# D's first key and query stacks made when their projections are complete, and the norms that begin a layer summing their squares on TensorE

## The chip, the cores and the metric

The kernel runs on one core of a Trainium2 chip. The metric is the device time of one execution in microseconds (us), lower is better. The engines of the core named here are TensorE (PE in the profile, with PEld for its weight loads), VectorE (DVE), ScalarE (ACT), GpSimd (POOL) and SyncE (SP), which here only issues DMAs.

## The reference

A trunk of two layers on 768 tokens of 1024 channels: 512 of a prompt and 256 of a sample, which don't see each other. All is fp32. One layer is, in the reference's own words:

```python
def _rmsnorm(x, gain):
    xf = x.astype(jnp.float32)
    xf = xf * lax.rsqrt(jnp.mean(xf * xf, axis=-1, keepdims=True) + EPS)
    return (xf * gain.astype(jnp.float32)).astype(x.dtype)
...
# sandwich RMSNorm -> one input projection split among four token mixers
#   A: 2-D neighbourhood attention with a learned position bias
#   B: grouped-query attention, normalised q and k, 2-D axial rotary positions
#   C: differential attention with ALiBi
#   D: sliding-window grouped-query attention, learned sink logit and ALiBi
# -> a projection per branch -> sigmoid gates, one per branch -> output projection
# -> post RMSNorm -> residual add; then a gated ConvFFN between two RMSNorms
```

D has four query heads of 64 channels and two key heads; a query sees keys at most 128 tokens away:

```python
logits = jnp.einsum('bqkgd,bskd->bkgqs', q_blk, k).astype(jnp.float32) * scale
logits = logits - sl[None, :, :, None, None] * rel.astype(jnp.float32)[None, None, None]
logits = jnp.where(valid[None, None, None], logits, NEG_INF)
sink_col = jnp.broadcast_to(sk[None, :, :, None, None], logits.shape[:-1] + (1,))
p = jax.nn.softmax(jnp.concatenate([logits, sink_col], axis=-1), axis=-1)[..., :-1]
```

## The kernel before, in words

**Data and products.** Channels lie on the 128 partitions, tokens along the free dimension. A norm works on one group of 256 tokens at a time (G0, G1, G2), as four tiles of 128 x 2 x 256 (two blocks of channels each; the profile writes 128x512). A product of two fp32 matrices is made of three passes with split operands: each operand is cut into a rounded high part (a copy on ACT) and what is left (a subtraction on DVE). So each weight, each normalised activation `h`, and each stack of keys or queries costs a copy on ACT and a subtraction on DVE before TensorE can use it. All products are issued by the helper at L460, transposes and broadcasts by transpose at L464, ACT's operations at L476, DVE's at L490, L494 and L499, the rsqrt on POOL at L505, DMAs at L509. A row with one of these lines is known by its tiles: `w` a weight, `raw` the same as loaded, `h` the activation, `g` general buffers (stacks, sums), `p` buffers of 128 x 512, `b` and `d` PSUM: four banks of 512 words (`b`) and two blocks of 1024 (`d`).

**A norm** (`pre_norm`, L713). ACT squares the four tiles of a group; DVE adds the second, third and fourth square to the first (three adds of 128 x 512); `mean_square` (L700) multiplies the sum by a column of ones on TensorE, four matmuls of 128 x 2 in fp32, which the profile shows as eight. DVE and POOL make the reciprocal root, TensorE spreads it over the partitions with two transposes, DVE multiplies the tiles by it, ACT copies them to `h` and DVE subtracts to get what is left. Six norms begin a layer: one for each of three token groups in the two layers. Layer 0's are made by `first_norm` (L760) from tiles loaded from DRAM. Layer 1's belong to the end of layer 0's FFN (`sandwich`, L772), where a first norm of the FFN's output, the residual add and the next layer's `pre_norm` follow one another. The other norms (inside a layer, before the FFN) go through the same `pre_norm` with `easy` set; the change leaves them as they are.

**A layer's attention part.** The list `JOBS` sets the order: first V of B and D with, in the same job, the keys of D and the first queries of D (`AHEAD`), one token group after another; then an early gate `t` (the first is A5: 48 products of 128x512 form of `h` with a weight from the bias buffers); then `job_D`, and the others. In `job_V` (L1797) the two blocks `k` and `q` of D are complete after G2 and put into `begun`; `proj` (L950) hands them out when `job_D` (L1864) asks for them, after the early gate. `job_D` then starts the tasks that make the stacks: `k_stack` (L985) copies each half of the block, subtracts, and sends the result to the other half of the partitions by DMA; `q_stack` is a copy and a scaled subtraction. Each of the two `d` blocks is free again when its stack is made. `job_D` then projects the second queries (q1) into a `d` block and starts the heads.

**What sets the order.** The order on each engine is not written out: a planner (class `Flow`, L243) runs the jobs as tasks at build time, with a clock per engine and a cost estimate per instruction, and emits an instruction whenever a task reaches it. A task with a lower number goes first; a `yield t` lets the task sleep until the planned time t. So a change to one task can move instructions of all later ones. On the chip, each engine runs its instructions in the order so written and waits on semaphores.

## Time and profile before

| what | value |
|---|---|
| median of 3 runs | 2510.05 us (2509.87 to 2511.64) |
| the profiled execution | 2509.31 us, its span 2507.5 us |
| mean granted TensorE clock | 0.993 |
| TensorE busy | 2451.6 us, 98% |
| VectorE busy | 1715.7 us, 68% |
| ScalarE busy | 1279.4 us, 51% |

The span goes from the first to the last instruction of the core; the execution's own time is 1.8 us longer. A row of the timeline is one instruction or a run of equal ones: start, length, engine, line, operation, tiles out<-in, shapes, count, and in brackets how long the engine stood idle before it and what released it. Lengths on TensorE overlap a little, since its matmuls are pipelined. The granted clock is a share of full speed: 1.00 is 2.4 GHz, 0.50 is 1.2 GHz.

### The profile page before, as it was taken

The page shows a single profiled execution, that of the slowest core. Times are in us where ns is not written, and L with a number is a line of the kernel's source. Part 1 is how long each engine was busy: PE and PEld are TensorE (multiplying, and loading weights), DVE is VectorE, ACT ScalarE, POOL GpSimd, SP SyncE. Part 2 cuts the span into 40 slices and gives each one's busy share as a digit, 9 for nine tenths or more (in the row PEclk, how much of TensorE's full clock was granted, in tenths as well). Part 3 has the DMA queues.
Part 4 walks back from the last instruction along what each step waited for, and adds up shares of the span by engine and source line. Part 5 has one row for each costly group of instructions (what it writes and reads, how often), then busy time and mean ns, then how long its engine had stood idle before and what let it go on. Part 6 is the DMA issues. An engine that isn't in the chain of part 4 may idle for free.

```text
span 2507.5 us, 40408 instructions
## 1 busy us (share of the span) xinstructions
PE 2451.6 (98%) x15486; PEld 2275.7 (91%) x15486; DVE 1715.7 (68%) x3278; ACT 1279.4 (51%) x2492; POOL 39.7 (2%) x38
## 2 busy tenths in 40 slices
PE   7999999999999999999989999999999999999998
PEld 7898888888999999988889988888889999999887
DVE  5567567736467888776766675676464679887866
ACT  5565655622355655563555645655224555556533
POOL 0001000000000000000000010000000000000000
PEclk9999999999999999999999999999999999999999
DMA  3443355343333333363334432544333233433643
GB/s 126 128 118 102 93 159 142 106 144 120 102 110 122 111 112 108 100 230 124 127 110 118 126 104 81 162 129 141 135 102 125 84 124 114 121 117 125 196 142 105
DMA packets 164273, 309.92 MB, mean 124 GB/s; under 512 B 25968, under 2 KB 90096, under 8 KB 164080
## 3 DMA queue, kind: packets, MB, share of 16 engines
q1 hardware_dynamic: 164080, 307.34, 39.7%
q8 instruction: 122, 2.00, 0.3%
q14 instruction: 71, 0.58, 0.1%
HBM read 225.74 MB, written 62.65 MB: 115 GB/s over the span
## 4 chain that ended last, share of the span: by engine, by line
PE 46%; DVE 2%; ACT 2%; issue 1%; DMA 1%; POOLq 0%; DVEq 0%; ACTq 0%
PE d L460 31%; PE b L460 15%; PE b L464 1%; DVE g L490 1%; ACT g L476 1%; DVE p L490 0%; DMA raw<-weights 0%; ACT p L476 0%; DVE h L490 0%; ACT s L476 0%; ACT w L476 0%; DVE w L490 0%; DMA bi<-alibi 0%; DVE bi L490 0%; ACT bi L476 0%
## 5 line engine op out<-in xcount | busy, mean ns | idle before, releaser
L460 PE MATMUL d<-h,w 128*128 128x256 f32 (+2 forms) x5400 | 989.9, 335 | 10.5 <-DVE g L490 8.7
L460 PEld LDWEIGHTS d<-h,w 128*128 128x128 f32 x5400 | 825.1, 190 | 103.1 <-issue 11.4
L460 PE MATMUL d<-g,w 128*128 128x256 f32 (+2 forms) x2547 | 443.7, 330 | 2.0 <-ACT g L476 1.5
L460 PEld LDWEIGHTS d<-g,w 128*128 128x128 f32 x2547 | 398.9, 188 | 33.0 <-ACT g L476 4.2
L490 DVE TENSOR_TENSOR w<-raw,w 128x1024 fp32r<-128x1024 f32 (+3 forms) x216 | 238.2, 1104 | 230.7 <-ACT w L476 224.5
L476 ACT ACTIVATE w<-raw 128x1024 fp32r<-128x1024 f32 (+3 forms) x216 | 206.8, 959 | 122.2 <-PE d L460 71.0
L476 ACT ACTIVATE p<-p,st 128x256 f32<-128x256 f32 (+2 forms) x288 | 175.0, 613 | 151.8 <-DVE st L499 94.5
L460 PE MATMUL b<-h,w 128*128 128x384 f32 (+2 forms) x1272 | 223.8, 330 | 0.0
L460 PEld LDWEIGHTS b<-h,w 128*128 128x128 f32 x1272 | 203.6, 188 | 10.3
L460 PE MATMUL b<-g,w 128*128 128x384 f32 (+2 forms) x1233 | 207.3, 322 | 0.0
L476 ACT ACTIVATE g<-d 128x384 f32<-128x384 f32 (+6 forms) x200 | 105.3, 534 | 185.6 <-PE d L460 157.6
L460 PEld LDWEIGHTS b<-g,w 128*128 128x128 f32 x1233 | 197.9, 189 | 1.6
L490 DVE TENSOR_TENSOR g<-g,b 128x512 f32<-128x512 f32 (+2 forms) x178 | 104.5, 599 | 66.0 <-PE b L460 45.8
L494 DVE SCALAR_TENSOR_TENSOR p<-g,par,p 128x511 f32<-128x511 f32 (+1 forms) x224 | 137.4, 615 | 8.9 <-ACT p L476 5.0
L476 ACT ACTIVATE p<-b 128x512 fp32r<-128x512 f32 (+3 forms) x172 | 91.9, 541 | 91.0 <-PE b L464 75.7
L490 DVE TENSOR_TENSOR p<-b,p 128x512 fp32r<-128x512 f32 (+1 forms) x162 | 100.3, 630 | 42.6 <-ACT p L476 41.8
L490 DVE TENSOR_TENSOR g<-g,d 128x768 f32<-128x768 f32 (+2 forms) x114 | 77.8, 686 | 70.1 <-PE d L460 70.1
L476 ACT ACTIVATE g<-p 128x512 fp32r<-128x512 f32 (+1 forms) x116 | 66.4, 574 | 93.4 <-DVE p L490 59.3
L460 PE MATMUL b<-g,g 128*128 128x512 f32 (+2 forms) x384 | 105.7, 346 | 5.4 <-DVE st L1157 3.6
L476 ACT ACTIVATE p<-g,par 128x512 f32<-128x512 f32 (+1 forms) x112 | 78.7, 703 | 50.3 <-DVE g L490 49.5
L1157 DVE CUSTOM_DVE_ANT_0 p<-b,bi 128x512 f32<-128x512 f32 (+2 forms) x144 | 81.6, 567 | 25.7 <-PE b L460 16.6
L460 PE MATMUL b<-p,g 128*128 128x256 f32 x576 | 95.8, 288 | 2.3 <-DVE p L490 1.5
(119 smaller groups left out, 3116.1 us busy)
## 6 DMA issues: line engine op xcount, KB each, us to landing
raw<-weights SPq DMA_DIRECT2D x206, 512.0 KB, 3.8
bi<-weights SPq DMA_DIRECT2D x48, 512.0 KB, 4.2
g<-g SPq DMA_DIRECT2D x128, 96.0 KB, 2.3
p<-v SPq DMA_DIRECT2D x44, 256.0 KB, 3.7
x<-g SPq DMA_DIRECT2D x36, 256.0 KB, 2.2
p<-x SPq DMA_DIRECT2D x36, 256.0 KB, 4.4
v<-p SPq DMA_DIRECT2D x28, 256.0 KB, 2.0
p<-x_in SPq DMA_DIRECT2D x24, 256.0 KB, 4.6
```

The costliest lines, as they stand in the source:

```text
L460: self.nc.tensor.matmul(out=out, lhsT=lhsT, rhs=rhs, start=start, stop=stop, skip_group_check=more)
L464: self.nc.tensor.transpose(out=out, in_=in_, identity=self.ident)
L476: self.nc.scalar.activation(out=out, in_=in_, func=func, **k)
L490: self.nc.vector.tensor_tensor(out=out, in0=a, in1=b, op=op)
L494: self.nc.vector.scalar_tensor_tensor(out=out, in0=a, scalar=s, in1=b, op0=op0, op1=op1)
L1157: nc.vector.tensor_tensor_reduce(out=p[:, :nkey], in0=s[:, :nkey], in1=bt, scale=1.0, scalar=init, op0=ALU.add, op1=ALU.max, accum_out=mx[ ...
```

## The change

Two things change. In `pre_norm` without `easy`, that is in the six norms that begin a layer, each square goes straight to TensorE as a `mean_square` of its own: four groups that accumulate into the same PSUM bank, in place of three adds on DVE and one group. And the stacks of D's keys and first queries are started inside `job_V`, when the last token group of their projection is through, in place of being handed to `job_D`; `job_D` keeps only the second queries.

```diff
--- before.py
+++ after.py
@@ -725,16 +725,19 @@
             if first:
                 yield t
             t = q.t = self.act(q.ap, ap, AF.Square, t, q.t)
-            if i:
-                if first:
-                    yield t
+            if not easy:
+                yield t
+                t = self.mean_square(b, q.ap, not i, i == len(x) - 1, t)
+                q.drop(t)
+            elif i:
                 t = sq.t = self.tt(sq.ap, sq.ap, q.ap, ALU.add, t, sq.t)
                 q.drop(t)
             else:
                 sq = q
-        yield t
-        t = self.mean_square(b, sq.ap, True, True, t)
-        sq.drop(t)
+        if easy:
+            yield t
+            t = self.mean_square(b, sq.ap, True, True, t)
+            sq.drop(t)
         yield t
         r = self.rstd_bcast(b, 2, t)
         tn = next(r)
@@ -948,8 +951,6 @@
         return out
 
     def proj(self, kind, name, m):
-        if (kind, name, m) in self.begun:
-            return self.begun.pop((kind, name, m))
         w = yield from self.weight((kind, name, m))
         blk = yield from self.dblock()
         blk.t = yield from self.mblock(self.whole(blk), w, self.h_rhs(self.h), KB)
@@ -1818,7 +1819,7 @@
                 blk.t = yield from self.mblock([(blk.cols(c0, c0 + GRP), c0, c0 + GRP)], w, self.h_rhs(self.h), KB)
                 if G == 2:
                     w.drop()
-                    self.begun[key] = blk
+                    self.f.start(self.queries_D(blk, 0) if n else self.keys_D(blk), 0)
         for w in ws:
             w.drop()
 
@@ -1861,26 +1862,21 @@
             blk = yield from self.proj("q", "B", m)
             self.f.start(queries(blk, m), 0)
 
+    def keys_D(self, blk):
+        ks = yield from self.k_stack(blk.full, blk.t, 6)
+        blk.drop(ks[1].t - 2000)
+        self.d_keys.extend(ks)
+
+    def queries_D(self, blk, m):
+        q = yield from self.q_stack(blk.full, 0.125, blk.t, 6)
+        blk.drop(q.t)
+        while not self.d_keys:
+            yield self.f.now + 200
+        self.heads("D", (2 * m, 2 * m + 1), lambda h: (q, self.d_keys[m], self.v["BD"][1], None))
+
     def job_D(self, _):
-        kbox = []
-
-        def keys(blk):
-            ks = yield from self.k_stack(blk.full, blk.t, 6)
-            blk.drop(ks[1].t - 2000)
-            kbox.extend(ks)
-
-        def queries(blk, m):
-            q = yield from self.q_stack(blk.full, 0.125, blk.t, 6)
-            blk.drop(q.t)
-            while not kbox:
-                yield self.f.now + 200
-            self.heads("D", (2 * m, 2 * m + 1), lambda h: (q, kbox[m], self.v["BD"][1], None))
-
-        blk = yield from self.proj("k", "D", 0)
-        self.f.start(keys(blk), 0)
-        for m in range(2):
-            blk = yield from self.proj("q", "D", m)
-            self.f.start(queries(blk, m), 0)
+        blk = yield from self.proj("q", "D", 1)
+        self.f.start(self.queries_D(blk, 1), 0)
 
     def job_C(self, m):
         part, m = m[0], int(m[1])
@@ -1898,7 +1894,7 @@
 
     def layer(self, l):
         self.l = l
-        self.begun = {}
+        self.d_keys = []
         self.par = self.pars[l]
         self.queue, self.bias_queue, self.att_end = [], [], False
         self.f.start(self.bias_loader(), 1)
```

The order shows three places. First ACT in layer 0 around the early gate A5 (the last row `p` <- `b` pair is A5's output, `d` are the blocks of D's keys and queries, `g` their stacks, `w` weights). Before:

```order
L476 ACTIVATE w_584<-raw_251 128x1024
L476 ACTIVATE lam_610<-lam_610 128x2
L476 ACTIVATE w_627<-raw_303 128x1024
L476 ACTIVATE w_650<-raw_590 128x1024
L476 ACTIVATE w_673<-raw_636 128x1024
L476 ACTIVATE p_685<-b_619 128x512
L476 ACTIVATE g_687<-d_287 64x768
L476 ACTIVATE g_691<-d_287 64x768
L476 ACTIVATE g_695<-d_335 64x768 x2
L476 ACTIVATE p_708<-b_620 128x256
```

and after:

```order
L476 ACTIVATE g_609<-d_323 64x768
L476 ACTIVATE g_613<-d_323 64x768
L476 ACTIVATE w_619<-raw_262 128x1024
L476 ACTIVATE lam_645<-lam_645 128x2
L476 ACTIVATE g_658<-d_360 64x768 x2
L476 ACTIVATE w_667<-raw_340 128x1024
L476 ACTIVATE w_696<-raw_625 128x1024
L476 ACTIVATE p_723<-b_654 128x512
L476 ACTIVATE p_737<-b_655 128x256
```

The copies of D's stacks stood behind A5's output and now stand ahead of it: k's two ahead of the weight copies, q's pair between them.

The second is the start of the program on TensorE (`const` with two columns: the sums of squares; `h_93` the first normalised activation, `st` the broadcast). Before:

```order
L460 MATMUL b_130<-const,p_131 128x2 x4
L464 MATMUL b_130<-const,st_146 128x128 x2
L460 MATMUL d_197<-w_157,h_93 128x256 x12
L460 MATMUL d_197<-w_179,h_93 128x256 x12
L460 MATMUL b_118<-const,p_119 128x2 x4
L460 MATMUL d_241<-w_157,h_93 128x256 x12
L460 MATMUL d_241<-w_179,h_93 128x256 x12
```

and after:

```order
L460 MATMUL b_130<-const,p_131 128x2 x4
L460 MATMUL b_130<-const,p_137 128x2 x4
L460 MATMUL b_130<-const,p_143 128x2 x4
L460 MATMUL b_130<-const,p_149 128x2 x4
L464 MATMUL b_130<-const,st_155 128x128 x2
L460 MATMUL b_118<-const,p_119 128x2 x4
L460 MATMUL b_118<-const,p_195 128x2 x4
L460 MATMUL b_203<-const,p_204 128x2 x4
L460 MATMUL d_219<-w_166,h_93 128x256 x6
L460 MATMUL b_118<-const,p_210 128x2 x4
L460 MATMUL d_219<-w_166,h_93 128x256 x6
L460 MATMUL d_219<-w_186,h_93 128x256 x6
```

One group for G0 became four; two groups of G1 (p_119, p_195) and one of G2 (p_204) now stand ahead of the first product of V (d_219).

ACT at the same place, where p_1xx and p_2xx are the squares and h_93 the copies of the activation. Before:

```order
L476 ACTIVATE w_157<-raw_106 128x1024
L476 ACTIVATE p_119<-p_110 128x512
L476 ACTIVATE h_93<-p_94 128x2x256
L476 ACTIVATE h_93<-p_96 128x2x256
L476 ACTIVATE h_93<-p_98 128x2x256
L476 ACTIVATE h_93<-p_100 128x2x256
L476 ACTIVATE p_165<-p_112 128x512
L476 ACTIVATE w_179<-raw_108 128x1024
L476 ACTIVATE p_185<-p_114 128x512
L476 ACTIVATE p_192<-p_116 128x512
```

and after:

```order
L476 ACTIVATE w_166<-raw_106 128x1024
L476 ACTIVATE h_93<-p_94 128x2x256
L476 ACTIVATE h_93<-p_96 128x2x256
L476 ACTIVATE h_93<-p_98 128x2x256
L476 ACTIVATE h_93<-p_100 128x2x256
L476 ACTIVATE p_119<-p_110 128x512
L476 ACTIVATE w_186<-raw_108 128x1024
L476 ACTIVATE p_195<-p_112 128x512
L476 ACTIVATE p_204<-p_120 128x512
L476 ACTIVATE p_210<-p_114 128x512
```

The squares of G1 and G2 moved behind the four copies of `h` and behind the second weight.

The third is the boundary of the layers on TensorE, at the norms of G1 and G2 (b with `const`: sums of squares; `b_13082`, `b_13111` and `b_13134`: V of G1). Before:

```order
L460 MATMUL d_12989<-h_11743,w_12842 128x256 x12
L460 MATMUL d_13031<-h_11743,w_12868 128x256 x7
L464 MATMUL b_12911<-const,st_12993 128x128 x2
L460 MATMUL d_13031<-h_11743,w_12868 128x256 x17
L460 MATMUL b_13082<-w_12282,h_11743 128x256 x12
L460 MATMUL b_13082<-w_12332,h_11743 128x256 x12
L460 MATMUL b_13111<-w_12282,h_11743 128x256 x12
L460 MATMUL b_13111<-w_12332,h_11743 128x256 x12
L460 MATMUL b_13056<-const,p_13057 128x2 x4
```

and after:

```order
L460 MATMUL d_13060<-h_11768,w_12905 128x256 x11
L464 MATMUL b_12941<-const,st_13024 128x128 x2
L460 MATMUL d_13060<-h_11768,w_12905 128x256
L464 MATMUL b_12774<-const,st_13030 128x128 x2
L460 MATMUL d_13060<-h_11768,w_12905 128x256 x12
L460 MATMUL b_13089<-const,p_13090 128x2 x4
L460 MATMUL b_13089<-const,p_13120 128x2 x4
L460 MATMUL b_13089<-const,p_13126 128x2 x4
L460 MATMUL b_13134<-w_12307,h_11768 128x256 x6
L460 MATMUL b_13089<-const,p_13132 128x2 x4
L460 MATMUL b_13134<-w_12307,h_11768 128x256 x6
L460 MATMUL b_13134<-w_12357,h_11768 128x256 x12
```

Three groups of G2's norm now stand ahead of V of G1, and one in the middle of it, where the only one stood behind two blocks of V.

And DVE there, where `p` as a second input is the old sum that is added. Before:

```order
L499 TENSOR_SCALAR st_12993<-b_12911 128x2
L490 TENSOR_TENSOR g_10899<-g_10899,b_12830 128x2x256
L490 TENSOR_TENSOR g_10950<-g_10950,b_12830 128x2x256
L490 TENSOR_TENSOR g_11006<-g_11006,b_12830 128x2x256
L490 TENSOR_TENSOR g_11057<-g_11057,b_12830 128x2x256
L490 TENSOR_TENSOR h_11743<-g_10899,h_11743 128x2x256
L490 TENSOR_TENSOR h_11743<-g_10950,h_11743 128x2x256
L490 TENSOR_TENSOR h_11743<-g_11006,h_11743 128x2x256
L490 TENSOR_TENSOR h_11743<-g_11057,h_11743 128x2x256
L490 TENSOR_TENSOR g_10899<-g_10899,b_12911 128x2x256
L490 TENSOR_TENSOR g_10899<-g_10899,p_12903 128x2x256
```

and after:

```order
L499 TENSOR_SCALAR st_13024<-b_12941 128x2
L499 TENSOR_SCALAR st_13030<-b_12774 128x2
L490 TENSOR_TENSOR g_10924<-g_10924,b_12941 128x2x256
L490 TENSOR_TENSOR g_10924<-g_10924,p_12933 128x2x256
L490 TENSOR_TENSOR g_10975<-g_10975,b_12941 128x2x256
L490 TENSOR_TENSOR g_10975<-g_10975,p_12935 128x2x256
L490 TENSOR_TENSOR g_11031<-g_11031,b_12941 128x2x256
L490 TENSOR_TENSOR g_11031<-g_11031,p_12937 128x2x256
L490 TENSOR_TENSOR g_11082<-g_11082,b_12941 128x2x256
L490 TENSOR_TENSOR g_11082<-g_11082,p_12939 128x2x256
L490 TENSOR_TENSOR g_10924<-g_10924,b_12774 128x2x256
L490 TENSOR_TENSOR g_10975<-g_10975,b_12774 128x2x256
```

Of the two norms that end together, the multiplications of G1's norm and its subtractions into `h` stood ahead of the pairs of multiply and add for G2; now the four pairs stand ahead.

## Rows read from the trace of the kernel before

**Rows 1.** The page: the span, and busy time of each engine.

```profile
span 2507.5 us, 40408 instructions
...
PE 2451.6 (98%) x15486; PEld 2275.7 (91%) x15486; DVE 1715.7 (68%) x3278; ACT 1279.4 (51%) x2492; POOL 39.7 (2%) x38
```

**Rows 2.** What TensorE waited for, whole span: total us, times, longest us.

```profile
PE b L460 <- DVE p L490: 21.3, 18, 8.6
...
PE d L460 <- DVE g L490: 9.1, 4, 4.2
```

**Rows 3.** Timeline of TensorE, layer 0: start, length, form, count [idle before, releaser].

```profile
60.61 8.64 PE L460 MATMUL b<-h,bi 128*128 128x512 f32 x48
...
73.43 4.93 PE L460 MATMUL d<-h,w 128*128 128x512 f32 x18 [4.17 <-DVE g L490]
...
80.77 4.67 PE L460 MATMUL d<-h,w 128*128 128x512 f32 x26
```

**Rows 4.** Timeline of TensorE, the same place in layer 1.

```profile
1305.16 8.64 PE L460 MATMUL b<-h,bi 128*128 128x512 f32 x48
...
1317.97 5.90 PE L460 MATMUL d<-h,w 128*128 128x512 f32 x18 [4.17 <-DVE g L490]
```

**Rows 5.** Windows on TensorE: us, busy (count), granted clock, DMA share, GB/s.

```profile
16.30:60.60 44.30, 41.01 (x307) 0.96 0.24 75
...
73.40:78.20 4.80, 4.77 (x18) 0.64 0.94 213
...
1228.40:1278.90 50.50, 44.18 (x326) 0.90 0.36 115
...
1278.90:1305.20 26.30, 24.51 (x204) 1.00 0.17 55
...
1318.00:1323.70 5.70, 5.70 (x18) 0.52 0.94 242
```

**Rows 6.** Timeline of the other engines beside A5, layer 0.

```profile
69.67 0.79 ACT L476 ACTIVATE g<-d 64x768 fp32r<-64x768 f32 x1
...
71.47 2.32 SPq L509 DMA_DIRECT2D g<-g  x2
...
75.14 0.96 DVE L494 SCALAR_TENSOR_TENSOR g<-d,g 64x768 fp32r<-64x768 f32 x1 [0.87 <-ACT g L476]
```

**Rows 7.** Timeline of the first 24 us.

```profile
2.76 0.47 SPq L509 DMA_DIRECT2D const<-const  x1
...
8.57 1.86 PE L460 MATMUL b<-const,p 128*128 128x2 f32 x8 [8.57 <-DVE p L490]
...
11.46 0.69 PE L464 MATMUL b<-const,st 128*128 128x128 f32 x2 [1.03 <-POOL st L505]
...
13.18 2.47 DVE L490 TENSOR_TENSOR p<-p,b 128x512 f32<-128x512 f32 x4
...
13.95 2.42 ACT L476 ACTIVATE h<-p 128x512 fp32r<-128x512 f32 x4 [1.43 <-DVE p L490]
...
16.31 4.54 PE L460 MATMUL d<-w,h 128*128 128x256 f32 x23 [1.10 <-DVE h L490]
...
21.45 1.05 PE L460 MATMUL b<-const,p 128*128 128x2 f32 x8 [0.59 <-DVE p L490]
```

**Rows 8.** Timeline of ACT in the same stretch.

```profile
16.28 0.61 ACT L476 ACTIVATE p<-p 128x512 f32<-128x512 f32 x1
...
16.80 1.04 ACT L476 ACTIVATE w<-raw 128x1024 fp32r<-128x1024 f32 x1
```

**Rows 9.** DMA issues of the first 60 us: count, KB each, us to landing.

```profile
const<-const SPq DMA_DIRECT2D x1, 72.0 KB, 4.5
```

**Rows 10.** Timeline of TensorE and DVE at the layer boundary.

```profile
1261.23 1.15 PE L460 MATMUL b<-const,p 128*128 128x2 f32 x8 [2.29 <-DVE p L490]
...
1278.97 0.68 DVE L490 TENSOR_TENSOR g<-g,b 128x512 f32<-128x512 f32 x1
...
1284.27 2.28 DVE L490 TENSOR_TENSOR p<-p,p 128x512 f32<-128x512 f32 x3
```

## The prediction

> **What bounds the kernel now.** I read the page first: TensorE is busy for 2451.6 us of a span of 2507.5 us [rows 1]. That is 55.9 us of idle time in all, so an edit that leaves TensorE's work alone can gain no more than that, and only at the place of a wait. The second view, TensorE's waits by releaser, names the places that the change is aimed at [rows 2]: 21.3 us in 18 waits for a DVE add that finishes a sum of squares (8.6 of it is the start of the program, before any product), and 9.1 us in four waits for the stacks. Then the timeline of TensorE around the early gate A5 in both layers [rows 3, 4], the windows view for the clock that was granted there [rows 5], and the rows of the stacks, the start and the layer boundary [rows 6 to 10]. The reader is to see that a wait of TensorE costs more than its own length where the granted clock falls after it: after 4.17 us of idle the 18 products that stand first in D's turn took 4.93 and 5.90 us, while 26 of the same form later took 4.67.
>
> **D's stacks made early.** Before, A5's 48 products run from 60.61 to 69.25 [rows 3], TensorE then stands, and the chain of copies and subtractions of D's stacks goes from 69.67 to 76.10 on ACT and DVE, with two DMAs on SP's queue, 2.32 us for both [rows 6]. Nothing of it needs A5; q1's products wait because they write into one of the two wide PSUM blocks (d) that the chain still reads. After, the chain of k stands ahead of A5 on ACT and DVE, beside the 24 products of q; q's chain stands beside A5's 8.64 us. So the second product group of D, q1's 24 products of which 18 stand together here, starts when A5 ends. Full speed is 4.67/26 = 0.18 us a product, 3.24 us for 18. Layer 0: from 69.25 to 78.20, the end of the 18, is 8.95 us, which becomes 3.24: 5.7 gained. Layer 1: 1313.80 to 1323.70 [rows 4, 5] is 9.9, less 3.24: 6.7 gained. Together 12.4 us. Only 2 x 4.17 = 8.3 of it is the wait itself; the other 4.1 is the clock, granted at a mean of 0.64 and 0.52 over the 18 products [rows 5]. So the bounds are 8.3 and 12.4, and I take 12.4, because the fall follows the idle time in both layers. What is late next: the DMA of the ALiBi rows, which can't start before A5 has freed their buffers. It is covered by the 24 to 28 products (about 5 us) that now stand behind A5; if it isn't, the wait that comes is some 2 us a layer, the length of the two DMAs in rows 6. The moved copies and subtractions are 4 + 4 instructions of 0.8 to 0.96 us a layer on engines that are idle for much of this stretch; they cost nothing there, hidden beside q's and A5's products.
>
> **Norms: what goes and what comes.** Six norms lose three DVE adds each: 18 x 0.76 (2.28 for three [rows 10]) = 13.7 us of DVE, an engine busy for 68% [rows 1]. They gain three groups of squares each on TensorE, 18 in all. A group is 8 instructions in the profile and takes 1.05 us with the overlap at its ends, 0.9 net of that, so 18 x 0.9 = 16.2 us on the engine that is the bound. That is more than all that the add-waits cost apart from the start; so the norms can only lose unless the DVE adds held TensorE for longer than the extra groups. I go through the two places.
>
> The Trainium skill, page "TensorE: Matmul & The Clock Gate", section "Back-to-back issue gap", gives matmuls of 1 to 64 columns an issue floor of about 25 ns. By it 18 x 8 products would take an estimated 3.6 us in place of 16.2, and the sum would be some 12 us lower. The row of this trace disagrees (8 in 1.05 us [rows 7]), and the row decides.
>
> **The start (layer 0).** The ones with which the squares are multiplied land at 2.76 + 4.5 = 7.26 us [rows 7, 9]; no group can start earlier. Before, one group ran from 8.57 to 10.43 at the start's slow pace (1.86 us) and the two transposes ran at 11.46. After, four groups of about 1.75 (that row less the overlap) stand there: 7.26 + 7.0 = 14.3, so the transposes come 3.9 us later, at 15.35. Half of that was slack (DVE was splitting a weight until 13.2), so the multiplications start at 16.1 instead of 13.18 and ACT's four copies of h end at about 19.3 instead of 16.37 [rows 7]. The order on TensorE then puts the first two groups of the second norm and the first of the third ahead of V's first product; their squares stand on ACT behind the four copies, with a weight copy between: 19.3 + 0.61 + 1.04 + 2 x 0.61 = 22.2 [rows 8], and the group of p_204, at the slow pace, ends near 24.1. V then starts at about 24.3 with everything else ready, where before it ran from 16.31 with waits. From there to A5: before 41.01 us busy and 3.29 idle [rows 5]; after, three more groups are left (2.7) and none of the waits: 24.3 + 41.01 + 2.7 = 68.0, against 60.6. So the start loses 7.4 us. Bounds: if V isn't held by the late squares for more than 3 us, and the groups take 1.05, then +4.6; lower still, +2, if some other order of arrival lets the third norm's square come early; with one more fall of the clock +9 (0.64 over 4.8 us [rows 5] is 3.5 us at the lower level, 1.7 us lost). I take +7.4.
>
> The skill's same page, section "Step-by-step: what each phase is for", says that the matmuls stay in program order and only weight loads are pulled ahead. If a ready product could pass a waiting group, V would start near 19.3 and the start would lose only some 2.4 us. The trace agrees with the page: at 1261.23 TensorE waits 2.29 us for a sum, with products of the next projection behind it [rows 10].
>
> **The layer boundary.** From 1228.4, where the first sum of squares of the boundary is through, to 1278.9, where V begins for the second token group, TensorE is busy for 44.18 and idle for 6.32 us, at a mean clock of 0.90 [rows 5], so about 5.0 of the busy time is loss by the clock: 39.1 us of work. After, 9 more groups stand in it (three more in each of two norms, and three of the third norm's four, whose only group was behind V): 39.1 + 8.1 = 47.2. The waits for the adds go, but two others come. One of about 1.3 us: a third square stands on ACT behind a weight copy of 1.04. And one of about 6.2 us: the third norm's second group needs its square, and this square waits behind DVE's four pairs of multiply and add (0.68 each, 5.3 with the overlap [rows 10]), four multiplications of the other norm (2.47, as at the start [rows 7]), and ACT's last copy and the square (0.7 + 0.63): 9.1 us after the transposes, while TensorE has some 3.0 us of its own work (12 products and a group) to put beside it. With about 1.9 for the clock after it, V starts 47.2 + 1.3 + 6.2 + 1.9 = 56.6 us after the start of the window, against 50.5: +6.1. From V to A5 the wait of 1.79 goes (26.30 less 24.51 [rows 5]) and 2.4 of slow clock comes: +0.6. The boundary loses 6.7 us. Bounds: without either new wait 47.2 against 50.5, -3.3; with two falls of the clock more, +10.
>
> **The rest.** The planner writes the whole order anew, so the attention units of both layers interleave in another way. No row gives a price. Apart from the two waits named above TensorE idles 55.9 - 21.3 - 9.1 = 25.5 us in the whole span [rows 1, 2]; moving some tenth of it in either direction is an estimate of 0 with 3 either way.
>
> **Sum.** -12.4 + 7.4 + 6.7 + 0 = +1.7 us on the profiled execution's 2509.3, 2511.0. The median of the runs is 2510.05, 0.7 above that execution, so I forecast 2511.8 us. Within 0.2% (5 us) is about what a measurement of this kernel can tell from no change.
>
> **Rivals.** (a) Faster: the squares come early. If the new wait at the boundary is 1 us instead of 6.2 (DVE's pairs finish before the transposes matter) and V at the start is held for only 3 us, the terms are -12.4 + 4.6 + 1.5 = -6.3, 2503.7 us. For it: DVE and ACT have 0.76 us less to do for each add dropped. Against it: the rows of the new order put the copies ahead of the squares. (b) Slower: the clock. Before, the clock fell behind waits of 1 to 4 us followed by two-column groups [rows 5]; now four such groups stand in a row at three places. If each leaves TensorE at the lower level (1.2 GHz) for 3.5 us, at the start and at two places of the boundary, that is 3 x 1.7 = 5.1 more: +6.8, 2516.9 us. It decides from the third such fall on. (c) D's wait doesn't go, since another (ALiBi rows, or a stack behind a weight copy on ACT) takes its place: +14.1, 2524.2 us. Against it: stacks need 6.4 us [rows 6] and have q's products and A5's 8.64 us to hide behind.
>
> **How the numbers follow.** The forecast, with its own range of 2505 to 2515, has 0.47; (a) 0.21; (b) 0.28; (c) 0.04. Of the forecast's share nearly all is within 0.2%. Faster by over 0.2%: 0.21, same 0.47, slower 0.32. The range goes from 2502 (the early squares, somewhat better) to 2520 (the clock, somewhat worse).
>
> **What would show it.** In the changed kernel's trace: no 4.17 us wait after A5 in either layer, and q1's first 18 products at 0.18 us each; V's first long run of products starting at 24 to 25 us and A5 at about 68; four groups in a row before 14.5 us; at the boundary a wait of 5 us or more on a square of the third norm, and A5 some 6 to 7 us later than before, relative to the end of the attention of layer 0. The prediction is wrong if V starts before 20 us, if the boundary's wait is under 2 us, or if the granted clock is at half for more than two stretches of the boundary.

## The result, and the profile of the changed kernel

The changed kernel takes 2526.52 us (median of 4 runs, 2523.91 to 2530.42) against 2510.85 us (4 runs, 2509.87 to 2514.77): ratio 1.0069, 95% interval 1.0057 to 1.0082. It is slower by some 16 us, above the range of 2502 to 2520. The profiled execution is the longest of its runs, 2530.42 us, so its rows carry some 4 us more than the median; the kernel before's profiled execution is 1.5 us under its median.

First the page of the changed kernel (span, then busy time), to be laid beside [rows 1]:

```profile
span 2528.6 us, 40652 instructions
...
PE 2477.3 (98%) x15630; PEld 2299.8 (91%) x15630; DVE 1703.2 (67%) x3260; ACT 1280.4 (51%) x2488; POOL 40.7 (2%) x38
```

TensorE is busy for 25.7 us more, VectorE for 12.5 us less. The 144 added instructions of the squares at 0.1 us would be some 15 us. The rest fits the lower clock: TensorE was busy at it for 53.3 us, in the kernel before for 32.7 (with the time ahead of the first record of the clock counted as lower; the reason stands at the start's rows below), and half of the difference is 10 us. What TensorE waited for, to be laid beside [rows 2] (us in total, times, longest):

```profile
PE b L460 <- ACT p L476: 11.0, 4, 5.8
PE b L460 <- DVE st L1158: 7.7, 5, 2.3
PE b L460 <- DMA const<-const: 7.2, 1, 7.2
PE b L460 <- DVE p L490: 5.1, 6, 1.9
```

The waits for the DVE sums fell from 21.3 to 5.1 us and those for D's stacks are gone from the list. In their place stand waits for a square on ACT and for the column of ones, and the waits for the attention's score step on DVE (`st`, the same step as L1157 in the kernel before) grew from 4.4 to 7.7 us.

The start, on TensorE (start, length, form, count, idle before and releaser), which answers to [rows 7]:

```profile
7.19 6.96 PE L460 MATMUL b<-const,p 128*128 128x2 f32 x32 [7.19 <-DMA const<-const]
16.11 0.69 PE L464 MATMUL b<-const,st 128*128 128x128 f32 x2 [1.96 <-POOL st L505]
20.61 5.28 PE L460 MATMUL b<-const,p 128*128 128x2 f32 x24 [3.81 <-ACT p L476]
25.75 1.63 PE L460 MATMUL d<-w,h 128*128 128x256 f32 x6
27.18 1.70 PE L460 MATMUL b<-const,p 128*128 128x2 f32 x8
...
33.01 5.87 PE L460 MATMUL d<-w,h 128*128 128x256 f32 x30
...
70.61 8.64 PE L460 MATMUL b<-h,bi 128*128 128x512 f32 x48
79.09 5.46 PE L460 MATMUL d<-h,w 128*128 128x512 f32 x30
...
87.94 0.50 PE L460 MATMUL b<-g,g 128*128 128x256 f32 x2 [1.75 <-DVE st L1158]
```

The ones land at 7.19, the four groups end at 14.15, TensorE stands behind a square of the second token group until 20.61, and V begins at 25.75. Its products still take 5.87/30 = 0.196 us at 33 us, where in the kernel before 24 of them took 3.11 us, 0.13 each, from 22.36 on. A5 begins at 70.61 instead of 60.61 [rows 3]. Behind A5 there is no wait and 30 products take 5.46 us, 0.18 each; but D's next scores then wait 1.75 us for DVE's step on the first ones, and 1.19 us in layer 1. DVE itself stood there for the ALiBi rows' DMA, in layer 0 and in layer 1:

```profile
87.26 0.62 DVE L1158 CUSTOM_DVE_ANT_0 p<-b,bi,par 128x384 f32<-128x384 f32 x1 [2.63 <-DMA bi<-alibi]
...
1339.90 0.62 DVE L1158 CUSTOM_DVE_ANT_0 p<-b,bi,par 128x384 f32<-128x384 f32 x1 [2.08 <-DMA bi<-alibi]
```

This DMA is issued behind A5, at 80.32 us.

The slow pace at the start is the lower clock. From start to start V's products take 0.213 us until 37.6 us and 0.120 from there on, and it is there that the trace's records of the clock begin, with full speed; the windows show 1.00 ahead of it because no record says otherwise. In the kernel before the same change of pace and the first record stand at 19.6 us.

The boundary, on TensorE:

```profile
1285.66 1.05 PE L460 MATMUL b<-const,p 128*128 128x2 f32 x8 [0.39 <-ACT p L476]
1292.54 3.57 PE L460 MATMUL b<-const,p 128*128 128x2 f32 x16 [5.82 <-ACT p L476]
1295.97 1.63 PE L460 MATMUL b<-w,h 128*128 128x256 f32 x6
1297.40 1.70 PE L460 MATMUL b<-const,p 128*128 128x2 f32 x8
...
1323.81 8.64 PE L460 MATMUL b<-h,bi 128*128 128x512 f32 x48
```

The foreseen wait for the third norm's second square is there, 5.82 us. On DVE the four pairs of multiply and add and then the other norm's multiplications (the row here, four in one) stand before ACT's copies, which stand before the squares on ACT. DVE:

```profile
1288.83 2.47 DVE L490 TENSOR_TENSOR g<-g,b 128x512 f32<-128x512 f32 x4
```
ACT, where the squares are the three that write `p`:

```profile
1289.54 2.42 ACT L476 ACTIVATE h<-g 128x512 fp32r<-128x512 f32 x4 [3.93 <-DVE g L490]
1291.87 1.66 ACT L476 ACTIVATE p<-g 128x512 f32<-128x512 f32 x3
```

To see where the time went, I compared at which time TensorE has done the same work in both traces: all products and transposes by their columns, without the sums of squares. At the ends of eight stretches the changed kernel lags by this much, in us; the step is what the stretch added.

| stretch (end in the kernel before) | lag | step | predicted |
|---|---|---|---|
| start, to A5 of layer 0 (60.6) | +10.0 | +10.0 | +7.4 |
| A5 and D (100) | +7.2 | -2.8 | -5.7 |
| attention and gates (686) | +11.5 | +4.3 | 0 |
| FFN (1227.5) | +11.8 | +0.3 | 0 |
| boundary, to A5 of layer 1 (1305.1) | +18.7 | +6.8 | +6.7 |
| A5 and D (1350) | +13.2 | -5.4 | -6.7 |
| attention and gates (1929) | +20.3 | +7.1 | 0 |
| FFN (2467) | +21.1 | +0.8 | 0 |

The two attention stretches are the large difference. In windows of 80 us at their end (us, TensorE busy, granted clock, DMA share, GB/s), the kernel before:

```profile
440.00:520.00 80.00, 77.84 (x475) 1.00 0.39 125
1690.00:1770.00 80.00, 78.54 (x470) 0.98 0.40 127
```

and the changed one:

```profile
440.00:520.00 80.00, 73.75 (x435) 0.96 0.37 118
1690.00:1770.00 80.00, 74.07 (x428) 0.94 0.37 115
```

There are 4 us more idle time in each, and a lower clock behind it. Most of it is at one place of each layer: from 460 to 480 us of the kernel before the lag goes from +3.1 to +9.9, from 1710 to 1770 from +9.1 to +17.5. In layer 0 on TensorE:

```profile
477.13 0.66 PE L464 MATMUL b<-const,g 128*128 128x128 f32 x4 [0.74 <-DVE g L1019]
478.80 0.50 PE L460 MATMUL b<-g,g 128*128 128x512 f32 x1 [1.01 <-DVE p L490]
...
482.58 0.58 PE L460 MATMUL b<-g,g 128*128 128x256 f32 x1 [2.29 <-DVE st L1158]
...
485.49 3.14 PE L460 MATMUL d<-g,w 128*128 128x512 f32 x10
```

A unit is one head's scores, softmax and sums for 256 queries. Between 475 and 485 us no projection product (`h`, `w`) stands between the units' own products, so TensorE goes at the pace of the units' chains on DVE and ACT; then the branch's ten products run at half pace, 0.31 us each.

### The profile page after: what moved, and what is told of

Same layout as the page of the kernel before. It is cut to its first block, busy times and chain, and to the rows that moved or that the text cites. A ratio compares the mean times of both kernels' runs of the same rounds, so it can differ in the third digit from the quotient of the medians.

```text
span 2528.6 us, 40652 instructions
## 1 busy us (share of the span) xinstructions
PE 2477.3 (98%) x15630; PEld 2299.8 (91%) x15630; DVE 1703.2 (67%) x3260; ACT 1280.4 (51%) x2488; POOL 40.7 (2%) x38
## 4 chain that ended last, share of the span: by engine, by line
PE 91%; DVE 3%; ACT 2%; DMA 1%; issue 1%; POOL 0%; POOLq 0%; SPq 0%; DVEq 0%; ACTq 0%
PE d L460 60%; PE b L460 28%; PE b L464 3%; DVE g L490 1%; ACT g L476 1%; ACT p L476 1%; ACT w L476 1%; DMA bi<-alibi 1%; DVE p L490 0%; DVE w L490 0%; DVE p L494 0%; DVE p L1158 0%; DMA raw<-weights 0%; ACT h L476 0%; DVE g L494 0%
## 5 line engine op out<-in xcount | busy, mean ns | idle before, releaser
L460 PE MATMUL d<-h,w 128*128 128x512 f32 (+2 forms) x5208 | 955.3, 334 | 0.0
L460 PEld LDWEIGHTS d<-h,w 128*128 128x128 f32 x5208 | 791.9, 189 | 87.3
L460 PE MATMUL d<-g,w 128*128 128x256 f32 (+2 forms) x2691 | 478.9, 334 | 1.3 <-ACT g L476 0.7
L460 PEld LDWEIGHTS d<-g,w 128*128 128x128 f32 x2691 | 426.2, 190 | 38.5 <-ACT g L476 3.5
L490 DVE TENSOR_TENSOR w<-raw,w 128x1024 fp32r<-128x1024 f32 (+4 forms) x218 | 240.4, 1105 | 208.3 <-ACT w L476 203.6
L476 ACT ACTIVATE w<-raw 128x1024 fp32r<-128x1024 f32 (+4 forms) x218 | 208.7, 960 | 127.2 <-PE d L460 72.0
L460 PE MATMUL b<-h,w 128*128 128x384 f32 (+2 forms) x1176 | 207.5, 330 | 2.9 <-DVE st L1185 2.9
L460 PEld LDWEIGHTS b<-h,w 128*128 128x128 f32 x1176 | 188.9, 188 | 11.7 <-issue 3.5
L490 DVE TENSOR_TENSOR g<-g,b 128x512 f32<-128x512 f32 (+2 forms) x178 | 104.5, 598 | 60.6 <-PE b L460 47.1
L460 PE MATMUL b<-g,g 128*128 128x384 f32 (+2 forms) x384 | 108.6, 352 | 10.8 <-DVE st L1158 7.7
```

The costliest lines, as they stand in the source:

```text
L460: self.nc.tensor.matmul(out=out, lhsT=lhsT, rhs=rhs, start=start, stop=stop, skip_group_check=more)
L476: self.nc.scalar.activation(out=out, in_=in_, func=func, **k)
L490: self.nc.vector.tensor_tensor(out=out, in0=a, in1=b, op=op)
```

## The experiments

Each was timed against the kernel before on the same chip; ratios are to that. The steps are read as in the table above, from one profiled execution each, and they scatter: seven of these kernels (e1, e3, e5, e6, e9, e10, e11) have the kernel before's order on TensorE at the boundary and 0 to +4.0 us there, and e2, with its order in the attention, has -3.9 and -0.1. A single step under some 4 us says little.

**Only the stacks (e1).** The changed kernel with the norms of before:

```diff
-            if not easy:
-                yield t
-                t = self.mean_square(b, q.ap, not i, i == len(x) - 1, t)
-                q.drop(t)
-            elif i:
+            if i:
+                if first:
+                    yield t
                 t = sq.t = self.tt(sq.ap, sq.ap, q.ap, ALU.add, t, sq.t)
...
```

> D's stacks early, all norms as in the kernel before. Theory of the ledger (what the trace after shows): the wait after A5 goes in both layers (-5.9 and -5.4 us up to the first scores) but 1.75 and 1.19 us come back as waits of D's first scores for DVE, and the attention's end loses some 5 us a layer, since the units are spent earlier and the last ones stand without products between them. Sum +1 to +4 us: 2512 to 2515. Rival, the prediction's term for this part: -12.4 us and an attention of 0, 2498. The PE idle near 480 and 1730 us is to be 3 us more than before if the ledger is right, with the norms innocent of it.

Measured: 2515.15 us against 2507.15, ratio 1.0032 (1.0021 to 1.0043): slower, by the part that was forecast to gain 12.4 us. The steps behind A5 are -3.7 and -5.1 us, those of the attention +5.3 and +3.4. TensorE's order of products in the attention is the changed kernel's, and so are its waits at the end, without any change in a norm:

```profile
466.72 0.50 PE L460 MATMUL b<-g,g 128*128 128x512 f32 x1 [1.01 <-DVE p L490]
...
470.50 0.38 PE L460 MATMUL b<-g,g 128*128 128x256 f32 x1 [2.30 <-DVE st L1155]
```

And DVE in that place, where three scalings (a TENSOR_SCALAR and two in one row) stand right before the score's step (L1155) for which TensorE waits:

```profile
467.91 0.48 DVE L499 TENSOR_SCALAR p<-p,st 128x512 f32<-128x512 f32 x1
468.42 1.42 DVE L494 SCALAR_TENSOR_TENSOR p<-p,st,p 128x512 f32<-128x512 f32 x2
469.75 0.68 DVE L1155 CUSTOM_DVE_ANT_0 p<-b,bi 128x512 f32<-128x512 f32 x1
```

DVE goes from 465.98 to 473.8 us with hardly a gap there. So the attention's loss belongs to the stacks' part, as the ledger (the table of steps above) had it, but the whole is 8 us slower, not 1 to 4. In its steps D's gain and the attention's loss cancel; what is left stands at the boundary (+3.0) and in the FFNs (+0.6 and +3.2), for which no cause is shown.

**Only the norms (e2).** The kernel before with the first part of the change's diff.

> Squares on TensorE in the six norms that begin a layer, D's stacks as in the kernel before. Ledger: +10 us at the start and +6.3 at the boundary, +16: 2526 to 2528, the attention as before. Rival, the prediction's sizes: +14.1, 2525. If the norms are also what spoils the attention's end, over 2533. The first products of V are to start at 25 to 26 us.

Measured: 2523.85 us, ratio 1.0067 (1.0055 to 1.0079), 16.7 us over. The steps are +10.5 at the start and +8.7 at the boundary, with the same waits (3.81 and 5.82 us); the attention is not later (-3.9 and -0.1). V began at 26.03. The norms alone cost all that the whole change costs. So the parts do not add up in the medians: 8.0 and 16.7 us apart, 15.7 together. Where the difference lies isn't shown.

**Stacks with one place of the norms (e3, e4).** e3 has the squares on TensorE at the start alone (`if first:` in place of `if not easy:`), e4 at the boundary alone (`if not easy and not first:`).

> D's stacks early, squares on TensorE only in layer 0's three norms at the start; the three at the layer boundary add on DVE as before. Ledger: the stacks-only time plus 10 us at the start, about 2523. Rival: if the slow start is made up for later (the time is lost in a stretch that has slack), as stacks only, 2513.

Measured: 2520.86 us, ratio 1.0052 (1.0040 to 1.0064); step at the start +9.3, at the boundary 0.

> D's stacks early, squares on TensorE only in the three norms at the layer boundary; the start as before. Ledger: the stacks-only time plus 6.3 us, about 2519, with a wait of 5.5 to 6.2 us for a square of the third norm. Rival: the wait came only because the whole program was late against the DMAs; then it is under 2 us here and the time is within 3 us of stacks only.

Measured: 2517.97 us, ratio 1.0039 (1.0027 to 1.0051); step at the boundary +6.8 (in e1 +3.0, where TensorE's order at the boundary is that of the kernel before), wait 5.83 us:

```profile
1280.76 3.58 PE L460 MATMUL b<-const,p 128*128 128x2 f32 x16 [5.83 <-ACT p L476]
```

Both terms of the norms stand where the rows of the order put them. That nothing of them is made up for later isn't shown: in medians the two places bring 5.7 and 2.8 us over e1, less than the steps say (10.1 and 3.8 over e1's), and the nine runs of e1 alone spread over 11 us.

**The first group alone (e12).** The whole change, but in layer 0 the second and third token groups add on DVE:

```diff
-            if not easy:
+            if not easy and not (first and G):
...
-        if easy:
+        if easy or (first and G):
```

> The whole change except that in layer 0 only the first token group squares on TensorE; the second and third add on DVE as before, so that V's first products stand directly behind the first norm. Theory (most of the start's 10 us comes from squares of the later groups that stand ahead of V): V's products start at 19 to 20 us and A5 3 to 4 us later than in the kernel before instead of 10; the whole is 6 to 7 us under the changed kernel, ratio 1.004. Rival (the start's loss is in the first norm's four groups at slow pace): within 2 us of the changed kernel, 1.007.

Measured: 2521.01 us, ratio 1.0051 (1.0038 to 1.0065), by the ratios some 4.5 us under the changed kernel, less than expected, and the two intervals overlap. TensorE at the start:

```profile
18.25 0.58 PE L460 MATMUL d<-w,h 128*128 128x256 f32 x1 [1.50 <-ACT h L476]
19.93 3.14 PE L460 MATMUL d<-w,h 128*128 128x256 f32 x13 [1.09 <-DVE h L490]
...
27.34 2.39 PE L460 MATMUL d<-w,h 128*128 128x256 f32 x18
...
62.99 8.64 PE L460 MATMUL b<-h,bi 128*128 128x512 f32 x48
```

A5 comes 2.4 us later than in the kernel before, not 10, so the theory holds for the start. The 7.6 us between are not the later groups' waits alone. In e12 the clock rises at 24.8 us (the products go from 0.213 to 0.120 us there, and the first record of the clock is there), in the changed kernel at 37.6. From 20.61 to 37.63 the changed kernel is busy without a gap, 17.0 us at the lower clock, which by estimate costs 8.5 us; in e12 the 5.2 busy us from 18.25 to 24.76 cost 2.6. So most of the 7.6 us is the clock that rose later.

When it rises isn't fixed by the order. Four executions have the same order on TensorE up to A5, and V begins within 0.35 us in all of them:

| kernel | V begins | clock rises | A5 begins | step |
|---|---|---|---|---|
| e13 | 25.82 | 32.2 | 68.20 | +7.6 |
| e3 | 25.69 | 36.2 | 69.95 | +9.3 |
| changed | 25.75 | 37.6 | 70.61 | +10.0 |
| e2 | 26.03 | 38.5 | 71.13 | +10.5 |

Each us of a later rise costs about half a us. What sets its moment in an execution isn't shown.

**Products to bring the pace up (e7, e8).** Products that nothing uses, before the first group and behind its transposes, in the whole change (e7) and in e5 (e8):

```diff
+            if warm and i == 0:
+                for _ in range(2):
+                    self.nc.tensor.matmul(out=b[:, 0:GRP], lhsT=ap[:, 0, 0:128], rhs=ap[:, 1], start=True, stop=True)
...
+        if warm:
+            for _ in range(9):
+                self.nc.tensor.matmul(out=b[:, 256:384], lhsT=self.ident, rhs=self.ident, start=True, stop=True)
```

> The whole change, with products added that nothing uses: two of 128x256 on the first tile of x before the first sum of squares, and nine of 128x128 on the identity behind the first two transposes, where TensorE idles. TensorE's order is else that of the changed kernel. Theory (the start loses 10 us and not 7.4 because TensorE stays at half pace until 38.7 us, as two-column groups and waits do not bring it up): the products from 21 us on run at 0.12 us instead of 0.20, and the time is 5 to 9 us under the changed kernel, ratio 1.003 to 1.005. Rival (the pace goes by time since the start, not by work): as the changed kernel, 1.007.

Measured: 2534.36 us, ratio 1.0106 (1.0092 to 1.0120), by the ratios 9 us over the changed kernel. It failed in two ways. The norm's multiplications on DVE waited for the added products, which write into the same bank, so V began at 29.34 instead of 25.75. And the pace rose but did not last: the added products end at 20.39, the clock's records have full speed from 20.20 to 23.61, and then, in the wait of 3.81 us, the lower level until 40.68:

```profile
16.41 3.98 PE L761 MATMUL b<-const 128*128 128x128 f32 x18
24.20 5.28 PE L460 MATMUL b<-const,p 128*128 128x2 f32 x24 [3.81 <-ACT p L476]
29.34 1.63 PE L460 MATMUL d<-w,h 128*128 128x256 f32 x6
```

The windows of that stretch (TensorE's columns as above):

```profile
20.20:23.60 3.40, 0.19 (x2) 1.00 0.00 0
23.62:40.60 16.98, 16.39 (x77) 0.50 0.43 140
40.70:60.00 19.30, 19.30 (x165) 1.00 0.10 28
```

So the rival, that the pace goes by the time since the start, is not borne out: products that were added ahead brought the clock up 17 us earlier than in the changed kernel, and it fell again in the wait. Whether full speed kept through the groups would have won the 5 to 9 us stays untested.

> e5 with the same kind of added products (two and six) at the start, whose norms are those of the kernel before. Theory: 2 to 4 us less than e5, since the kernel before runs its first 24 products at half pace until 19.6 us. Rival: the added products delay the first sum by as much as they bring, as e5.

Measured: 2509.05 us, ratio 1.0003 (0.9994 to 1.0012), as e5, which was the rival's time, but not by its reason. The first sum isn't delayed (8.00 us against 8.17 in e5). V's first product is (15.65 against 14.20), and the clock, up at 20.16, was at the lower level again from 23.58 to 26.99 and from 40.64 to 44.06, which e5's records don't have. A5 begins 3.0 us later than in e5.

**When D's units enter the queue (e5, e6, e10, e11).** The stacks are early as in e1, the norms as before; only the moment is changed at which D's first attention units may be taken by the planner's workers. e5 waits for the second query's projection, the others for a time in the planner's clock after D's turn begins (`d_go`), 4, 2 and 6 us (here e11's):

```diff
     def queries_D(self, blk, m):
...
+        if not m:
+            while not self.d_go:
+                yield self.f.now + 200
+            yield self.d_go + 6000
         while not self.d_keys:
...
     def job_D(self, _):
+        self.d_go = self.f.now
...
```

> As e1 (stacks early, norms as before), but D's first attention units go into the queue only when the second query's projection is made. This order ends the attention as the kernel before does (TensorE's row equal from about product 3500 of layer 0 on), while the stacks still stand beside A5. Theory (the loss is in how the last units meet the last projections): the -4.3 and -5.9 us of the stacks stay, the +7.5 us a layer at the attention's end goes, 7 to 12 us under the kernel before: ratio 0.995 to 0.997. Rival (early stacks spend units early, whatever the order at the end): as e1, ratio 1.003.

> As e1, but D's first units go into the queue 4 us of the planner's clock after D's turn begins: a shift of the same kind as e5, whose order at the attention's end is that of e1 and not that of the kernel before. Theory: the wait after A5 is gone, yet the idle time of some 5 us near 465 and 1715 us is there again and the time is that of e1, ratio 1.002 to 1.005. Rival (a later start of the units is what cures): as e5, below 1.

> As e6 with 2 us in place of 4; the order at the attention's end is again that of the kernel before, as in e5. Theory: the stacks' gain of 4 to 8 us a layer up to 100 us after the layer's start, less what bare places cost: one or two a layer, ratio 0.997 to 1.002. If the time of start alone decided, it would lie between e1 (1.003) and e6 (1.0035).

> As e6 with 6 us in place of 4, a third order. Theory as for e10: ratio 0.997 to 1.002, and the number of idle times of 2 us and more in the attention (with half clock behind each) tells which. Rival: later units are better units, so below e5's 1.000.

| kernel | median, before | ratio (95%) | D, layers 0 and 1 | attention, layers 0 and 1 | start, boundary and FFNs |
|---|---|---|---|---|---|
| e1, at once | 2515.15, 2507.15 | 1.0032 (1.0021 to 1.0043) | -3.7, -5.1 | +5.3, +3.4 | +6.0 |
| e10, 2 us | 2509.11, 2508.99 | 0.9999 (0.9990 to 1.0008) | -5.1, -5.4 | +1.7, +5.7 | +2.6 |
| e6, 4 us | 2517.36, 2508.27 | 1.0035 (1.0023 to 1.0047) | -6.2, -6.1 | +5.7, +10.1 | +4.8 |
| e11, 6 us | 2503.04, 2508.99 | 0.9978 (0.9968 to 0.9987) | -4.7, -5.4 | +0.1, +2.5 | +4.5 |
| e5, after q1 | 2507.81, 2508.27 | 1.0000 (0.9991 to 1.0009) | -6.5, -7.0 | +5.2, +7.1 | -2.0 |

Behind A5 all five gain 3.7 to 7.0 us a layer, where the prediction had 5.7 and 6.7. All but e11 give most of it back or more in the attention, at one or two places where TensorE finds only units. The expectation of e5 was wrong: its attention ends in the order of the kernel before (TensorE's rows are equal from 517 us on), and yet it loses ahead of that, at two places. One is near 475 us, again a wait of 2.48 us for DVE; the other is near 230 us, where units wait for DVE, which is busy almost without a gap from 228.5 to 234.2 us (TensorE's window, columns as above):

```profile
222.00:242.00 20.00, 16.59 (x88) 0.83 0.27 65
```

e6 came out as expected: the wait for scores behind A5 is gone (0.49 us is left in layer 1) and the idle time at the attention's end is as large as e1's (2.21 and 3.56 us). e11 has one such wait of 1.24 us a layer, and its windows at the attention's end are these:

```profile
432.00:512.00 80.00, 76.47 (x462) 0.98 0.35 116
1683.00:1763.00 80.00, 76.40 (x455) 0.98 0.34 111
```

It is faster than both kernels, by 0.22% of the kernel before. The time of the queue isn't a rule (2 us is better than 4, 6 better than 2); the waits come with the order that it brings. e11 was found as the best of five; e13 below times its order of the attention a second time.

**The same shift without any early stack (e9).** The kernel before, D's first units 2 us later:

```diff
             while not kbox:
                 yield self.f.now + 200
+            if not m:
+                yield self.f.now + 2000
```

> The kernel before, with D's first units put into the queue 2 us of the planner's clock later and nothing else: no work added, removed or made early; the wait of 4.17 us after A5 stays. TensorE's order of the units in the attention changes by half all the same. Theory (where units meet bursts of DVE is what the planner leaves to chance, and each meeting costs 2 to 3 us of idle and as much by the clock): another time than before by 4 to 10 us, most likely slower, ratio 1.002 to 1.004, with new idle times of 2 us and more in the attention. Rival (the attention is insensitive to such shifts, and the loss of e1 is due to the stacks' early work on ACT and DVE): ratio within 0.001 of 1.

Measured: 2512.94 us against 2508.99, ratio 1.0012 (1.0002 to 1.0022): some 3 us slower, less than the 1.002 to 1.004 of the theory and just past the rival's 0.001. The profiled execution, 2.2 us shorter than the kernel before's, shows steps of -1.2 and +1.2 us in the attention, and no new wait of 2 us. So a mere shift of units costs little here. That the loss of e1 is chance alone, as the theory had it, is not shown; nor is it that the stacks' early work is needed for it.

**The whole change with e11's order (e13).**

> The whole change, norms included, with e11's later start of D's first units; its attention is in e11's order. Theory (two separate losses: the norms' +16 us at the start and the boundary, and the attention's +4 to +7 us a layer, which is an order of the units and can be had away): about 12 us under the changed kernel, the start still +10 and the boundary still +6 to +7, the attention +0 to +3 a layer; ratio to before 1.002 to 1.0035. Rival (with the norms' delay the attention loses whatever the order): as the changed kernel, 1.006 to 1.007.

Measured: 2515.52 us against 2507.86, ratio 1.0034 (1.0022 to 1.0045): half of the change's loss. Steps: start +7.6, D -4.7 and -5.4, boundary +7.4, attention -2.5 and -0.2, in the shortest of its seven runs. So the attention's loss can be had away while the norms stay.

## Why the prediction was wrong

- **The sum, and the step that failed.** "0 with 3 either way" for the rest. The rest cost +4.3 and +7.1 us in the attention and 1.1 in the FFN, 12.5 together (some 2.6 us of it by the pace told of below). e1 shows the attention's part without the norms (+5.3 and +3.4), e2 shows none of it with the norms alone, and in another order it is gone (e13) or mostly so (e11). In runs: the stacks' part, forecast to gain 12.4 us, lost 8.0 by itself. I had priced the attention's order by a tenth of the idle time in the whole trace; the row that should have been read is the window at its end, where the kernel before already had idle time in the midst of units that stand alone. What fails there is known, TensorE left with units alone that wait for DVE; why the early stacks bring the units into that order, and a shift alone (e9) hardly does, stays open.
- **D's wait.** The wait of 4.17 us and the slow products behind it went, as foreseen: 0.18 us a product in both layers. What is late next was named rightly, the ALiBi rows' DMA, but taken to be covered. Its price was read from the 2.32 us of the two issues in [rows 6]; here its two transfers took 6.9 us from issue to landing (median), more than the about 5 us of products that were to cover it. DVE stood 2.63 and 2.08 us for it and TensorE behind DVE 1.75 and 1.19, with the clock at half for 3.4 us behind the first (mean 0.88 from 79.1 to 92.9 us). 8.2 us were gained of 12.4 at this place; in e5 and e6, whose first units come later, 13.5 and 12.3.
- **The start.** Right in its mechanism and low in its size: +10.0, against +7.4 with a bound of +9. V began at 25.75 and not 24.3; and the clock stayed at the lower level until 37.6 us, for 12 us of V's products and groups, where I had taken over the share of before (3.3 us from V on and 3.4 us near 40). The step itself ranges from +7.6 to +10.5 with the moment at which the clock rises. That a group that waits holds up ready products was right, but the row at 1261.23 does not show it, since the products behind it stood 0.31 us more for DVE. The changed kernel does: with the same first norm V's first product ran at 18.25 in e12, and here, behind three groups, at 25.75.
- **The boundary.** +6.8 against +6.7, the wait 5.82 against 6.2. e4 shows the wait without the start's norms. That the sizes agree to 0.1 us is luck, since steps at this place scatter by up to 4 us.
- **The groups' price.** 0.95 us a group (1.70 at the slow pace) against 0.9. The trace bore out the row and not the 25 ns floor of the Trainium skill's page "TensorE: Matmul & The Clock Gate", section "Back-to-back issue gap": 24 instructions of two columns took 5.28 us at the start, 8 of them 0.95 elsewhere.
- **The rivals.** None of them was the case as a whole. (b) had the sign, and the clock was indeed lower for longer at the start, but the attention, where most was lost, isn't in it. (c) came nearest with 2524.2 us, by luck: D's wait did go, and what took its place, the ALiBi rows that (c) names, cost 1.75 and 1.19 us. The rows do not tie the falls of the clock to two-column groups, as (b) has it: of the kernel before's five falls up to 1330 us (at 40.1, 74.2, 1262.1, 1275.7 and 1316.7) three came in or behind waits that no two-column group followed. None of the signs of being wrong that the prediction named for itself occurred (V at 25.75, the wait 5.82, one stretch of half clock at the boundary): all three watch the norms, none the attention.

## What to carry to other kernels

A wait that is removed ahead of a stretch whose order a planner writes is a gain only once that stretch has been followed to its end: look there for the places where the busiest engine has only work that hangs on other engines, and price the gain as given back until the order is shown not to meet them. An operation moved onto the engine that bounds the kernel must be asked two things: what it takes there (here 18 groups of 0.95 us, 17 us) and which ready work its own operands hold up in program order (here two new waits, 3.81 and 5.82 us, and a clock that rose later). And where an order is found by a planner, try a few starts of the moved work before judging the move: the same stacks were 0.35% slower (e6) and 0.22% faster (e11).

## What the runs showed that I had not expected

TensorE at full granted clock, with no idle time, runs the same alternation of 512 and 256 column products at two paces that hold over a long stretch. Here is the gates' stretch of layer 1 in the kernel before (window, TensorE busy, granted clock, DMA share, GB/s),

```profile
1810.00:1830.00 20.00, 20.00 (x117) 1.00 0.45 138
```
and the changed one:

```profile
1830.00:1850.00 20.00, 20.00 (x115) 1.00 0.50 165
```

117 products in 20 us are 171 ns each, 115 are 174. Taken from start to start in the trace, the product of 512 columns takes 230 ns in the one and 237 in the other, that of 256 columns 117 in both. Over the 150 us of this stretch 1.7% is some 2.6 us, for the same instructions; in layer 0 both kernels run it at the slower pace. It explains a part of the last attention step of +7.1. The order of the products doesn't set it: e1, whose products stand in the changed kernel's order, takes 230 ns here. What does is open.
